# Query and key products by seven: order of the tiles in a bank, order of the jobs, place of the attention

## The chip, the cores and the metric

The kernel runs on one core of a Trainium2 chip. The metric is the device time of one execution in microseconds, the median of several runs. A core has engines with a queue of instructions each: TensorE (PE in the profile; PEld is its weight load), VectorE (DVE), ScalarE (ACT), GpSimd (POOL) and SyncE (SP), which here only issues transfers between the chip's main memory and the core's working memory. An engine works through its queue in order; where an instruction needs another engine's result it waits for a semaphore, and everything behind it in its queue waits too. TensorE writes its results to PSUM, a memory of eight banks of 128 x 512 fp32 values, and VectorE and ScalarE read them from there.

## The reference

One layer of a hybrid decoder, 512 positions, width 1024, all in fp32:

```python
u = rmsnorm(x, ln1_g[i])
proj = u @ w_in[i]
q, k, v, pool_in, z, xbc, dt_raw, gate_pre = jnp.split(proj, split_idx, axis=-1)
y_a = dilated_attention_mixer(q, k, v, rel_bias) @ w_a[i]
y_b = pool_mixer(pool_in, pool_w[i], pool_scale[i]) @ w_b[i]
y_c = ssd_mixer(z, xbc, dt_raw, ssd_conv_w[i], ...) @ w_c[i]
merged = gates[:, :, 0] * y_a + gates[:, :, 1] * y_b + gates[:, :, 2] * y_c
x = x + merged @ w_o[i]
x = x + conv_ffn(rmsnorm(x, ln2_g[i]), ...)
return rmsnorm(x, final_g)
```

The attention has three groups of six heads of 64 columns; group 0 looks back without gaps, group 1 at every fourth position, group 2 at every sixteenth. The change concerns the queries and keys of group 1: 384 columns of `w_in` each, so two products of 512 x 1024 by 1024 x 384.

## The kernel before, in words

**Three products for one.** A product in fp32 is made of three: each operand is split into a high part (fp32r) and the remainder, and high by high, high by low and low by high are added in PSUM (`mm3`, L228). For the weights, ScalarE casts the high part (`wh`, L195) and VectorE subtracts it from the raw weights to get the low one (`wl`, L215). The matmuls that use `wl` come last in a tile.

**Jobs.** All work with weights is a list of jobs, written by hand in `program()` (L1473). A job has a load, a cast, a split and a body of matmuls. The main loop (L1684 on) does this before the body of job n: the split of the weights of n+1, the cast for n+2, the fetch for n+3. The cast is cut in two and its halves are issued in the body's steps. There are two buffers of raw weights, three of high parts, two of low parts. TensorE, VectorE, ScalarE and GpSimd do their instructions in the order of the program; SyncE's order is left to the scheduler of the framework, which may take a transfer that is ready ahead of one that is not.

**Steps.** `step()` (L156) issues the pending half of a cast and lets side work go on one piece: a list of waiting items, one taken up per step, among them the heads of the attention, which `attend(g)` (L725) puts there. An attention item does its scores in the step that takes it up, its softmax on VectorE and ScalarE, its transposes two steps later and its output product after that.

**Seven products for eight.** The product of group 1's queries and keys is cut in quarters (rows of the weights even and odd by blocks of 128, columns query and key; positions in two halves) and computed by seven quarter products of sums and differences instead of eight (`qk_sevens`, L647): one, two, five, three, six, seven, four. The sums of `u` are in `US`; the sums of weights are made on VectorE (`diff`, L338) in place: `W[0]` and `W[1]` are two quarters loaded on their own (L657), and `W[0]` becomes `W[0]` less one's weights, `W[1]` becomes `W[1]` less the new `W[0]`. Five takes its weights from `W[0]`, three and six from `W[1]`, one, two, seven and four have loads of their own.

A job of `qk_sevens` has three tiles c = 0, 1, 2 of 128 columns by 256 positions, 12 matmuls each. A bank of PSUM takes two such tiles: tiles 0 and 1 share a bank, tile 2 has the first half of a second one. X and Z (tag `sm`, four banks in all) and Y (tag `mm`) are pairs of banks. One writes X, two Y, five Z; three adds to Z, and six, seven and four add to X. After each tile its reader runs: a copy to working memory on ScalarE (L696 for one and five, L705 for six) or a sum on VectorE (L700 for two, L706 for six, L709 for seven); three is not read. The framework keeps two engines off the same bank: a matmul into one half waits for a read of the other half that was issued before it.

**The order around it.** Before the change the list runs: value product of groups 1 and 2, also by seven (`v_pair`, whose results SyncE copies into place, `vr<-v`, L624), then one gate job (two tiles of 512 positions), the seven query/key jobs, attention of group 1, one more gate job, and the six jobs (twelve tiles) of the convolution's input (`xbc_evac`, L901).

Of the kernel before, what the change touches and what calls it, by code (L numbers as in the profile page):

```python
# [13 lines left out]
OP = mybir.AluOpType  # L14
# [69 lines left out]
def trunk(ctx: ExitStack, tc, out, x, rel_bias, ln1_g, w_in, b_gate, w_a, pool_w, pool_scale, w_b,  # L84
# [3 lines left out]
    act, dve, pool, pe, sp = nc.scalar, nc.vector, nc.gpsimd, nc.tensor, nc.sync  # L88
# [19 lines left out]
    def T(name, dt=F32, shape=(P, S)):  # L108
        return big.tile(list(shape), dt, name=name, tag="t")
# [228 lines left out]
    def diff(out, a, b):  # L338
        dve.tensor_tensor(out, a, b, OP.subtract)  # L339
        return out  # L340
# [70 lines left out]
    def side_u(j):  # L411
        if j in QUARTER:
            two, half = QUARTER[j]
            return [(uh[:, 2 * p + two, half], ul[:, 2 * p + two, half]) for p in range(4)]
        return [US[j, p] for p in range(4)]
# [154 lines left out]
    def grouped(ap, g):  # L570

        return ap.rearrange("p (r j) -> p r j", r=4)[:, :, ::-1]
# [4 lines left out]
    def plain(ap, g):  # L577
        return ap if g == 0 else ap.rearrange("p (r j) -> p r j", r=4)
# [68 lines left out]
    def qk_sevens(g):  # L647

        cols = (C_Q + 384 * g, C_K + 384 * g)
        q = lambda two, h: w_in[:, cols[h]:cols[h] + 384].rearrange(  # L650
            "(k two p) c -> two p k c", two=2, p=P)[two]
        W, X, Z, Y, r1, r5 = [], {}, {}, {}, {}, {}

        def load():
            for h in range(2):
                W.append(ypool.tile([P, 4, S], F32, name="w3", tag="xs")[:, :, :384])
                sp.dma_start(W[h], q(h, 1))  # L657

        def at(banks, c):
            return banks[c // 2][:, (c % 2) * 256:(c % 2) * 256 + 256]  # L660

        def half(which, c, hi):
            if (which, g, c) not in QK:
                QK[which, g, c] = T(f"{which}{g}")
            t = QK[which, g, c]
            t = grouped(t, g) if which == "q" else plain(t, g)
            return t[:, :, 64 * hi:64 * hi + 64]

        def turned_(ap):
            return ap.rearrange("p (j r) -> p r j", r=4)  # L670

        def job(source, j, banks, name, use, form=None):
            def body(ws):
                wh, wl = ws
                parts = side_u(j)
                for c in range(3):
                    fresh = name is not None
                    if fresh and c % 2 == 0:
                        banks[c // 2] = (MM if banks is Y else SM)(name)
                    cs = slice(c * P, (c + 1) * P)  # L680
                    mm3(at(banks, c), lambda k: wh[:, k, cs], lambda k: wl[:, k, cs],
                        lambda k: parts[k][0], lambda k: parts[k][1], range(4),
                        fresh and c % 2 == 0, True, again=not fresh or c % 2 == 1)
                    use(c)
                    if c != 1:
                        step()
            new = Job([source] if source is not None else [], 4, 384, body)
            new.form = form
            if source is None:
                new.load = lambda: None  # L690
            return new

        def keep(r, name, banks, scale):
            def use(c):
                r[c] = T(name)[:, :256]
                act.mul(r[c], at(banks, c), scale)  # L696
            return use

        def p2(c):
            dve.scalar_tensor_tensor(half("q", c, 0), turned_(at(Y, c)), 0.125, turned_(r1[c]),  # L700
                                     OP.mult, OP.add)

        def p6(c):
            r = T("r2")[:, :256]
            act.copy(r, at(X, c))  # L705
            dve.tensor_tensor(half("k", c, 0), turned_(at(Z, c)), turned_(r), OP.add)  # L706

        def p7(c):
            dve.tensor_tensor(half("k", c, 1), turned_(at(X, c)), turned_(r5[c]), OP.add)  # L709

        def p4(c):
            act.mul(half("q", c, 1), turned_(at(X, c)), 0.125)

        one = job(q(0, 0), "A11", X, "p1", keep(r1, "r1", X, 0.125))
        one.then = lambda: diff(W[0], W[0], one.raw)
        two = job(q(1, 0), "A12", Y, "p2", p2)
        five = job(None, 1, Z, "p5", keep(r5, "r5", Z, 1.0), lambda: W[0])
        three = job(None, 4, Z, None, lambda c: None, lambda: W[1])
        three.then = lambda: diff(W[1], W[1], W[0])
        six = job(None, 2, X, None, p6, lambda: W[1])  # L720
        seven = job(q(0, 0), 3, X, None, p7, lambda: diff(seven.raw, W[1], seven.raw))
        four = job(q(1, 0), "A22", X, None, p4, lambda: diff(four.raw, four.raw, W[1]))
        return load, [one, two, five, three, six, seven, four]

    def attend(g):  # L725
        nm, ls = both[:, :, :HEADS], both[:, :, 32:]
# [265 lines left out]
    btok, cb, prev, done = {}, {}, {}, set()  # L992
# [166 lines left out]
    def gate_jobs(b, lo=0, hi=8):  # L1159
        def evac(m, ps):  # L1160
            s = SG[b, lo + m] = T("sg")
            o = o_bg + 8 * b + lo + m
            act.activation(s, ps, AF.Sigmoid, bias=col[:, o:o + 1])  # L1163
            if b == 1:
                dve.tensor_tensor(MG[lo + m], MG[lo + m], s, OP.mult)

        return jobs_a(w_in, C_GATE + b * D + lo * P, hi - lo, uhk, ulk, KD, evac)
# [305 lines left out]
    def program():  # L1473
        yield from jobs_a(w_in, C_POOL, 8, uhk, ulk, KD, pool_evac)
        yield Call(lambda: waiting.append(rows_of_bias()))
        yield from v_jobs(0)
        yield from qk_jobs(0)
        yield from pool_out_job()
        yield Call(lambda: attend(0))
        yield Call(lambda: waiting.insert(3, ssd_prep()))  # L1480
        for i, job in enumerate(branch_jobs(1, w_b, YB, 8, more=range(7))):
            if i == 3:
                yield Call(lambda: running.extend(after(p, sums_of_u(p)) for p in range(4)))
            yield job
        load, pair = v_pair()
        yield Call(load)
        yield from gate_jobs(1, 0, SPLIT)
        load, keys = qk_sevens(1)
        for i, job in enumerate(pair):
            yield job  # L1490
            if i == 5:
                yield Call(load)
        yield from gate_jobs(1, SPLIT, SPLIT + 2)
        yield from keys
        yield Call(lambda: attend(1))
        yield from gate_jobs(1, SPLIT + 2)
        yield from jobs_a(w_in, C_XBC, 12, uhk, ulk, KD, xbc_evac)
        yield Call(ssd_start)
        yield from qk_jobs(2)
        yield Call(lambda: attend(2))  # L1500
        yield Call(lambda: fill([after(2, combine())]))
        yield from gate_jobs(0)
        many = {"a": branch_jobs(0, w_a, AO, 3), "g": gate_jobs(2),
                "Z": z_jobs(0), "z": z_jobs(1)}
        for token in MIX:
            if token in many:
                yield next(many[token])
            else:
                yield Call(lambda i=int(token): waiting.append(y_norm(i)))
        yield Call(finish)  # L1510
        yield from branch_jobs(2, w_c, YT, 8, last=True)
        yield Call(load_x1)
        for pair in range(2):
            for h in range(2):
                yield from wo_jobs(pair, h)
            if pair == 0:
                yield Call(ff_cols)
        first, between, _ = sevens_down(0)
        second_, last_, opened = sevens_down(1, keep=True)
        extra = {EARLY + i: between[w] for i, w in enumerate(  # L1520
            ("two", "one", "five", "three", "six", "seven", "four"))}
        extra.update({LATE + i: last_[w] for i, w in enumerate(("two", "one", "five", "six"))})
        for i, job in enumerate(up_jobs()):
            yield job
            if i == EARLY - 3:
                yield Call(first)
            if i == LATE - 1:
                yield Call(second_)
            if i in extra:
                yield extra[i]  # L1530
        yield Call(lambda: fin.setdefault("g", grow(final_g)))
        yield Call(finish)
        yield from down(last_, opened)
# [87 lines left out]
    for tb in range(2):  # L1621
        s0, s1, v, sq, r, rt = (small(n, [P, 1]) for n in ("s0", "s1", "v", "sq", "r", "rt"))
# [25 lines left out]
    r = rstd_of(ss, 2, D)  # L1648
# [68 lines left out]
SPLIT = 4  # L1717
# [33 lines left out]
```

## Time and profile before

| what | us |
|---|---|
| median of 3 runs | 1046.34 (1044.05 to 1047.76) |
| the profiled execution, its own time | 1045.46 |
| its span, first to last instruction | 1043.5 |
| TensorE busy | 1024.7 |
| VectorE busy | 690.7 |
| ScalarE busy | 475.1 |
| the seven query/key jobs, first to last matmul's start | 247.26 to 287.64 in the span |

How to read it: an engine's busy time is the sum of its instructions. A row of the timeline has the start and the length of one instruction or of a few alike, the engine, the line of the kernel, the operation, what it writes and reads, its shape and count; in brackets how long the engine had stood before it and whose result ended that. Matmuls are pipelined: one's length overlaps the next, so the distance of two starts says what a matmul takes. Names of tiles are shown without digits: p1, p2 and p5 are all `p`. Rows with "SPq" are issues of transfers.

### The profile page before, as it was taken

To read this page: it belongs to the slowest core of one execution; us is meant where nothing else is said; L and a number is where in the kernel's file an instruction comes from. 1 tells how busy PE (TensorE), PEld (TensorE's weight loads), DVE (VectorE), ACT (ScalarE), POOL (GpSimd) and SP (SyncE) were. 2 spreads that over 40 slices of the span, in tenths; PEclk is the share of its full clock that TensorE was granted. 3 is DMA by queue.
4 is the path that set the end of the run, shared out by engine and by line. 5 is a ranking of instruction groups with operands and counts; after the bars stand their busy time and mean duration, and the time that the engine had idled before them with its cause. 6 is when DMAs were issued, how large, how long until landed. Compare 5 with 4: busy or idle time off the path is not lost.

```text
span 1043.5 us, 13347 instructions
## 1 busy us (share of the span) xinstructions
PE 1024.7 (98%) x5312; PEld 864.2 (83%) x5312; DVE 690.7 (66%) x921; ACT 475.1 (46%) x778; POOL 149.4 (14%) x125
## 2 busy tenths in 40 slices
PE   9999999998899999999999999999999999999997
PEld 9998878897788878888888888898888888888885
DVE  5563566685647657767677755767677776666775
ACT  5432544443355354565564333545445344453342
POOL 1670000000000004310134500001110000111120
PEclk9999999999999999999999999999999999999999
DMA  7444312045232235342244535443223324323142
GB/s 262 138 126 138 115 48 74 31 122 161 83 120 81 81 101 162 96 149 79 81 131 140 173 104 210 164 142 110 93 81 122 119 72 173 121 81 121 61 142 81
DMA packets 115996, 122.34 MB, mean 117 GB/s; under 512 B 5315, under 2 KB 98310, under 8 KB 115935
## 3 DMA queue, kind: packets, MB, share of 16 engines
q1 hardware_dynamic: 115343, 120.64, 35.8%
q8 instruction: 42, 0.69, 0.3%
q10 hardware_dynamic: 592, 0.86, 0.2%
q14 instruction: 19, 0.16, 0.0%
HBM read 117.69 MB, written 2.22 MB: 115 GB/s over the span
## 4 chain that ended last, share of the span: by engine, by line
PE 92%; DVE 3%; ACT 2%; DMA 1%; issue 1%; SPq 1%; ACTq 0%; DVEq 0%
PE pa L234 34%; PE pu L234 22%; PE pb L234 10%; PE p L234 9%; PE pqk L234 6%; PE pa L1602 2%; PE ps L748 1%; PE pu L1404 1%; DVE wl L215 1%; PE ppw L234 1%; PE pt L776 1%; PE po L789 1%; PE py L1074 1%; DMA xin<-in_x_dram 1%; ACT wh L195 1%
## 5 line engine op out<-in xcount | busy, mean ns | idle before, releaser
L215 DVE TENSOR_TENSOR wl<-raw,wh 128x2048 fp32r<-128x2048 f32 (+3 forms) x96 | 218.5, 2278 | 49.9 <-ACT wh L195 42.3
L195 ACT CAST wh<-raw 128x1024 fp32r<-128x1024 f32 (+3 forms) x190 | 189.5, 1017 | 66.0 <-DVE raw L339 36.4
L1265 DVE SCALAR_TENSOR_TENSOR hc<-pu,fcol,hc 128x510 f32<-128x510 f32 x88 | 65.8, 747 | 61.2 <-ACT hc L1262 59.6
L234 PE MATMUL pa<-uh,wh 128*128 128x512 f32 x384 | 98.6, 399 | 0.0
L234 PE MATMUL pa<-ul,wh 128*128 128x512 f32 x384 | 94.9, 389 | 0.0
L234 PE MATMUL pa<-uh,wl 128*128 128x512 f32 x384 | 94.9, 389 | 0.0
L234 PEld LDWEIGHTS pa<-ul,wh 128*128 128x128 f32 x384 | 72.1, 188 | 15.2
L234 PEld LDWEIGHTS pa<-uh,wl 128*128 128x128 f32 x384 | 72.1, 188 | 15.0
L234 PE MATMUL pu<-uh,wl 128*128 128x512 f32 (+1 forms) x352 | 83.7, 380 | 0.0
L234 PE MATMUL pu<-uh,wh 128*128 128x512 f32 (+1 forms) x352 | 83.6, 379 | 0.0
L234 PE MATMUL pu<-ul,wh 128*128 128x512 f32 (+1 forms) x352 | 83.5, 379 | 0.0
L234 PEld LDWEIGHTS pa<-uh,wh 128*128 128x128 f32 x384 | 70.2, 188 | 14.6 <-issue 0.7
L234 PEld LDWEIGHTS pu<-uh,wl 128*128 128x128 f32 x352 | 64.1, 188 | 12.7 <-DVE wl L215 0.3
L234 PEld LDWEIGHTS pu<-ul,wh 128*128 128x128 f32 x352 | 64.2, 188 | 12.4
L234 PEld LDWEIGHTS pu<-uh,wh 128*128 128x128 f32 x352 | 64.1, 188 | 12.4
L1270 POOL TENSOR_TENSOR hc<-hc 128x512 f32<-128x512 f32 x22 | 30.4, 1381 | 278.9 <-DVE hc L1265 243.9
L1262 ACT ACTIVATE hc<-pu,fcol,fcol 128x512 f32<-128x512 f32 x40 | 31.2, 780 | 82.6 <-PE pu L234 82.3
L1036 POOL TENSOR_TENSOR xd<-xc,dec 128x512 f32<-128x512 f32 x6 | 6.4, 1062 | 341.6 <-DVE xc L1030 322.7
L769 ACT ACTIVATE sb<-sb,both 128x128 f32<-128x128 f32 (+1 forms) x72 | 30.1, 419 | 29.1 <-DVE both L766 18.9
L1163 ACT ACTIVATE sg<-pa,col 128x512 f32<-128x512 f32 x24 | 16.5, 687 | 50.4 <-PE pa L234 43.7
L1267 ACT ACTIVATE hc<-hc 128x512 f32<-128x512 f32 x22 | 13.9, 632 | 42.7 <-DVE hc L1265 42.6
L912 DVE SCALAR_TENSOR_TENSOR xs<-pa,col,xs 128x509 f32<-128x509 f32 (+2 forms) x24 | 18.0, 749 | 17.0 <-ACT xs L908 16.5
(376 smaller groups left out, 1867.0 us busy)
## 6 DMA issues: line engine op xcount, KB each, us to landing
raw<-in_w_in_dram SPq DMA_DIRECT2D x25, 1024.0 KB
raw<-in_ffn_w_up_dram SPq DMA_DIRECT2D x22, 1024.0 KB
raw<-in_ffn_w_down_dram SPq DMA_DIRECT2D x11, 1024.0 KB
raw<-in_w_o_dram SPq DMA_DIRECT2D x8, 1024.0 KB
raw<-in_w_in_dram SPq DMA_DIRECT2D x14, 512.0 KB
raw<-in_w_in_dram SPq DMA_DIRECT2D x8, 768.0 KB
raw<-in_w_b_dram SPq DMA_DIRECT2D x4, 1024.0 KB
al<-ad SPq DMA_DIRECT2D x16, 256.0 KB
```

Of the source, the lines that this page charges most:

```text
L195: act.copy(job.high[:, :, o], job.raw[:, :, o])
L215: (eng or dve).tensor_tensor(l[:, :, o], job.raw[:, :, o], h[:, :, o].bitcast(F32), OP.subtract)
L234: pe.matmul(ps, l, r, start=first and n == 0, stop=last and n == total - 1, skip_group_check=again)
L748: pe.matmul(pss[i][:, o:o + w * P], q[r, n * P:(n + 1) * P], k[r, kb * P:(kb + w) * P], start=True, stop=True)
L769: act.activation(sb[:, off:off + w * P], sb[:, off:off + w * P], AF.Exp, bias=nm[:, n, h:h + 1], accum_out=ls[:, n, h:h + 1])
L912: dve.scalar_tensor_tensor(t[:, sh:], ps[:, :S - sh], col[:, o_cw + 12 * k + m:o_cw + 12 * k + m + 1], t[:, sh:], OP.mult, OP.add)
L1163: act.activation(s, ps, AF.Sigmoid, bias=col[:, o:o + 1])
L1262: act.activation(t, ps, AF.Identity, bias=ff["c1"][:, ff["b"] + m:ff["b"] + m + 1], scale=fw(2, m))
L1265: dve.scalar_tensor_tensor(t[:, sh:], ps[:, :S - sh], fw(k, m), t[:, sh:], OP.mult, OP.add)
L1267: act.activation(t, t, AF.Silu)
L1270: pool.tensor_tensor(a, a, t, OP.mult)
L1602: pe.matmul(first[2 * n + j][:, lo:hi], a[:, k, j * P:(j + 1) * P], b[:, k, lo:hi], start=a is wh and b is uh and k == 0, stop=a is wl and ...
```

## The change

In the body of a job of `qk_sevens`, tiles 0 and 1 are computed, then both are read, then a step is taken; tile 2 is computed and read and a second step is taken. Before, each tile was read right behind its matmuls and the first step came after tile 0. In seven, each tile is first copied to working memory by ScalarE, and VectorE's sum reads the copy. The jobs come as one, five, two, three, then the gate job, six, the second gate job, seven, four. Attention of group 1 starts behind four as before, but no gate job follows it: the convolution's jobs do.

```diff
@@ qk_sevens, body of a job
                         fresh and c % 2 == 0, True, again=not fresh or c % 2 == 1)
-                    use(c)
-                    if c != 1:
+                    if c:
+                        for done in (0, 1) if c == 1 else (2,):
+                            use(done)
                         step()
@@ qk_sevens, the reads
         def p7(c):
-            dve.tensor_tensor(half("k", c, 1), turned_(at(X, c)), turned_(r5[c]), OP.add)
+            r = T("r7")[:, :256]
+            act.copy(r, at(X, c))
+            dve.tensor_tensor(half("k", c, 1), turned_(r), turned_(r5[c]), OP.add)
@@ qk_sevens, what it returns
-        return load, [one, two, five, three, six, seven, four]
+        return load, [one, five, two, three], [six, seven, four]
@@ program
-        load, keys = qk_sevens(1)
+        load, begun, ended = qk_sevens(1)
         for i, job in enumerate(pair):
             yield job
             if i == 5:
                 yield Call(load)
+        yield from begun
         yield from gate_jobs(1, SPLIT, SPLIT + 2)
-        yield from keys
+        yield ended[0]
+        yield from gate_jobs(1, SPLIT + 2)
+        yield from ended[1:]
         yield Call(lambda: attend(1))
-        yield from gate_jobs(1, SPLIT + 2)
         yield from jobs_a(w_in, C_XBC, 12, uhk, ulk, KD, xbc_evac)
```

## The prediction

> **What bounds the kernel now.** I read the page's head and its chain first, then who waits for whom on TensorE, then the stretch that the change touches. On the page the first two lines are the span and TensorE's busy time, the third is the end of the chain.
>
> ```profile
> span 1043.5 us, 13347 instructions
> PE 1024.7 (98%) x5312; PEld 864.2 (83%) x5312; DVE 690.7 (66%) x921; ACT 475.1 (46%) x778; POOL 149.4 (14%) x125
> ...
> PE 92%; DVE 3%; ACT 2%; DMA 1%; issue 1%; SPq 1%; ACTq 0%; DVEq 0%
> ```
>
> TensorE carries the end: whatever delays its queue delays the kernel, other engines count only where TensorE waits for them. All its waits between 236 and 400 us are these:
>
> ```profile
> PE p L234 <- ACT r L696: 2.3, 3, 1.5
> PE p L234 <- DVE q L700: 2.1, 1, 2.1
> PE p L234 <- DVE k L709: 1.7, 1, 1.7
> PE p L234 <- ACT r L705: 1.6, 2, 1.1
> PE pcb L1005 <- ACT xcv L1093: 1.0, 1, 1.0
> PE p L234 <- ACT q L712: 0.5, 1, 0.5
> ```
>
> Columns: total, times, longest. Five of the six rows, 8.2 us in eight waits, are matmuls of the tiles p1 to p5 waiting for a reader in the group-1 query/key product, the function edited. By stretch (length, then busy time of TensorE, its weight loads, VectorE, ScalarE): one gate job, the seven products, the next gate job.
>
> ```profile
> 236.34:247.26 10.92, 10.92 (x49) 9.02 (x49) 6.18 (x6) 2.16 (x3) 0.00 (x0) 1.00 0.64 204
> 247.26:287.64 40.38, 32.24 (x253) 30.61 (x252) 23.55 (x20) 16.34 (x27) 0.00 (x0) 1.00 0.32 102
> ```
>
> The gate job is dense. The products are not, and TensorE's rows in order of time show how (start, length, operation, idle before and its releaser):
>
> ```profile
> 250.34 0.74 PE L234 MATMUL p<-uh,wh 128*128 128x256 f32 x4 [1.49 <-ACT r L696]
> ...
> 251.87 0.64 PE L234 MATMUL p<-uh,wh 128*128 128x256 f32 x4
> ...
> 253.31 0.64 PE L234 MATMUL p<-uh,wh 128*128 128x256 f32 x4
> ...
> 276.25 0.74 PE L234 MATMUL p<-sbh,wh 128*128 128x256 f32 x4 [1.15 <-ACT r L705]
> ...
> 279.63 0.74 PE L234 MATMUL p<-sbh,wh 128*128 128x256 f32 x4 [1.69 <-DVE k L709]
> ...
> 284.67 0.74 PE L234 MATMUL p<-uh,wh 128*128 128x256 f32 x4 [0.47 <-ACT q L712]
> ```
>
> A tile of 12 matmuls unhindered takes 253.31 - 251.87 = 1.44 us. The tile at 250.34 is the second half of a bank whose first half ScalarE was reading: it waited though the columns are different. The tile at 251.87, another bank, did not. So the half just written is read while the other half's matmuls stand still, in six of the seven jobs (three has no read), and two more waits stand where a job begins on a bank read late.
>
> **The change, part by part.** *Both halves first, then both reads.* The seven jobs hold 21 tiles; 21 x 1.44 = 30.24 us of the 40.38. The excess, 10.14 us, is what waits cost in start times: the 8.2 us of wait rows, and the restart after each (0.74 instead of 0.64 us for its first four, and a drained array). In the new order no read lies between the two tiles of a bank, so all six mid-bank waits go. I take off 10.14 and add back what is late next.
>
> Three ways of counting differ here. The stretch less busy matmul time gives 40.38 - 32.24 = 8.14 us to win, the starts give 10.14; I take the starts, since they include the restarts. The Trainium skill, "Perfetto Trace Analysis", section "Identifying the Most-Contended Engine", says that matmul busy time misleads, because pipelined instructions look smaller in the trace, and that weight-load time is the better measure; by it the window is 40.38 - 30.61 = 9.77 us, nearer to the starts, and the forecast would be 0.4 us slower.
>
> *The two waits at a job's start* (six's read before seven, 1.15 us; five's before three). Five and three now have two between them, 4.3 us of other banks; six and seven have a gate job of 10.92 us between. Cost nothing, covered by those; without the cover about the old 1.15.
>
> *Seven's copy.* Three more ScalarE reads of 128x256 from PSUM, priced by their likes:
>
> ```profile
> L705 ACT COPY r<-p x3: 364/372/374, 271.5 to 276.1; 128x256 f32<-128x256 f32 x3
> L709 DVE TENSOR_TENSOR k<-p,r x3: 605/624/626, 279.0 to 282.8; 128x256 f32<-128x256 f32 x3
> ```
>
> That is 3 x 0.37 = 1.1 us on an engine 16.34 us busy in 40.38. VectorE's three additions stay at most at 0.62 each. Seven and four remain neighbours on one bank: seven's two reads take 0.7 us and run under seven's third tile (1.44 us), so four starts unhindered; were ScalarE inside a cast (0.83 us, below) when they are due, four would wait about 0.1. Bounds 0 and the old 1.7; I take 0, as the casts are queued behind the reads.
>
> *The step after the first tile moves behind the second.* A step issues half a weight cast for the job two ahead, which now enters ScalarE's queue behind two reads, one tile (1.44 us) later. That matters only where a split is already short, next.
>
> *The order: one, five, two, three, gate, six, gate, seven, four.* One now follows the value product directly, at 236.34 instead of 247.26, and five follows one. This is the new price; VectorE, ScalarE and SyncE in that place:
>
> ```profile
> 235.28 2.28 DVE L215 TENSOR_TENSOR wl<-raw,wh 128x2048 fp32r<-128x2048 f32 x1
> 237.48 1.01 DVE L619 TENSOR_TENSOR v<-r,pb 128x384 f32<-128x384 f32 x2
> 243.08 1.76 DVE L215 TENSOR_TENSOR wl<-raw,wh 128x1536 fp32r<-128x1536 f32 x1 [4.59 <-ACT wh L195]
> 244.76 1.75 DVE L339 TENSOR_TENSOR w<-w,raw 128x1536 f32<-128x1536 f32 x1
> ...
> 229.56 3.47 ACT L195 CAST wh<-raw 128x768 fp32r<-128x768 f32 x4 [3.55 <-DVE raw L339]
> 241.48 1.57 ACT L195 CAST wh<-raw 128x768 fp32r<-128x768 f32 x2 [8.45 <-DMA raw<-in_w_in_dram]
> 247.86 0.83 ACT L195 CAST wh<-raw 128x768 fp32r<-128x768 f32 x1 [4.23 <-DMA raw<-in_w_in_dram]
> ...
> 219.51 0.37 SPq L183 DMA_DIRECT2D raw<-in_w_in_dram  x1
> 220.13 5.66 SPq L624 DMA_DIRECT2D vr<-v  x8
> 227.82 2.04 SPq L657 DMA_DIRECT2D w<-in_w_in_dram  x2
> 230.55 5.99 SPq L624 DMA_DIRECT2D vr<-v  x8
> 236.64 0.53 SPq L183 DMA_DIRECT2D raw<-in_w_in_dram  x1
> 237.27 4.93 SPq L624 DMA_DIRECT2D vr<-v  x8
> 242.30 0.53 SPq L183 DMA_DIRECT2D raw<-in_w_in_dram  x1
> 242.93 5.68 SPq L624 DMA_DIRECT2D vr<-v  x8
> ```
>
> One's weights take the raw buffer that the gate's had, so they are fetched at 219.51 and cast by 233. VectorE splits them at 235.28 where it split the gate's: 1.76, done 237.04. TensorE uses the low parts last, after 8 of 12 matmuls: 236.34 + 0.96 = 237.30. In time, by 0.26.
>
> Five's weights are W[0] less one's. W[0] and W[1] are issued by 229.86; a fetch of the same 768 KB took 241.48 - 236.64 = 4.84 us, so they are there by 234.7. The subtraction runs 236.96 to 238.7, the two value additions behind it end at 239.7 (nobody waits for them but the copies vr, needed by attention much later), ScalarE casts by 238.77 + 1.57 = 240.34, VectorE splits by 242.15. TensorE reaches five at 236.34 + 4.32 = 240.66, its low parts at 241.62. Short by 0.55, and with a restart 0.8 us. This is the one term I add; its ends are 0, if VectorE comes to the split half a microsecond sooner, and 2.1, the longest wait the stretch has shown.
>
> Two's weights come in the buffer free when the last value job is split, issued at 236.64 and landed 241.48 as one's did. ScalarE's cast of them, in two halves around one's third read, ends near 243.5; split by 245.3. TensorE, now 0.8 late, starts two at 245.8: in time. Three: cast behind five's reads by 247.1, split by 248.9, needed at 250.1. The gate job's fetch comes next in SyncE's queue at 242.30 and has until 254.4. From there each product has a gate job's 10.92 us of slack.
>
> *Attention moves behind four.* The gate job that hid its first two items now runs before, so its seven entries begin in the convolution's first tile, with 12 steps instead of 14 before the scan. The last entry is taken at step 7 and works at step 9: it fits. VectorE there:
>
> ```profile
> 302.72 2.28 DVE L215 TENSOR_TENSOR wl<-raw,wh 128x2048 fp32r<-128x2048 f32 x1
> 306.32 2.31 DVE L912 SCALAR_TENSOR_TENSOR xs<-pa,col,xs 128x509 f32<-128x509 f32 x3 [1.32 <-ACT xs L908]
> 308.55 0.68 DVE L762 TENSOR_TENSOR sb<-ps,b 128x512 f32<-128x512 f32 x1
> 309.27 0.69 DVE L766 TENSOR_REDUCE both<-sb 128x4 f32<-128x512 f32 x1
> 309.87 0.68 DVE L777 COPY sb<-pt 128x512 f32<-128x512 f32 x1
> ```
>
> A tile's share is 2.31 + 2.28/2 + 0.68 + 0.69 + 0.68/2 = 5.2 us, against 10.92/2 = 5.46 us of its matmuls and the attention's own beside them. It fits, narrowly; cost nothing, and without that cover about one copy per tile, 0.3 us each.
>
> **Sum.** 10.14 - 0.8 = 9.3 us. The profiled execution is listed at 1045.46 us, so 1036.1; the median before is 0.9 higher than that execution. I forecast 1036.5.
>
> **The rivals.** *Two's fetch falls behind the third group of copies* (SyncE takes it at 242.30 instead of 236.64). For it: the copies are ahead of it in the code. Against: at 219.51 a fetch was issued ahead of copies that the code puts first, whichever was ready earlier going first, and two's buffer is free before those copies' data. Price: landed 247.1, cast and one's third read 0.83 + 0.38 + 0.83 to 249.2, split to 250.9, where the low parts were due at 246.8; with a restart some 4.3 us. Time 1040.8.
>
> *The stretch turns out paced by ScalarE and VectorE.* VectorE's 23.55 us and the chain cast, split, difference stay, in 31 us instead of 40.38; then each wait removed returns before a weight and the time stays near 1045. For it, the narrow margins above. Against, the value product just before:
>
> ```profile
> 207.20:236.34 29.14, 29.14 (x169) 29.14 (x168) 24.38 (x25) 13.63 (x20) 0.00 (x0) 1.00 0.38 116
> ```
>
> There VectorE is busy 24.38 of 29.14 us and TensorE never stops.
>
> *Slower: W[0] and W[1] are issued late.* In the old order one's weights, not W[0], came last, so nothing shows that W is early enough when five follows one. Issue to usable split is 4.84 + 1.75 + 1.57 + 1.76 = 9.92 us; needed at 241.62. Issued behind the third group of copies, 242.30, five waits 10.6 us and the gain is gone (1045.9). Behind the fourth, 248.6, it waits 16.9: 1045.5 - 10.1 + 16.9 = 1052.3. It decides from an issue at 241.8 on. Against it, the row at 227.82, with the same buffers free at the same time. The Trainium skill, "TensorE: Matmul & The Clock Gate", section "What's actually happening", adds that after an idle window of about 3.4 us the clock falls to half for as long: an estimate from it is 1.7 us on top; no wait in this stretch is long enough to show it, and the granted clock in its rows is 1.00.
>
> **How the numbers follow.** Forecast 0.70, range 1034 to 1038.5 (0 to 2 us of small waits, and the runs' spread); late fetch of two 0.16; no gain 0.06; slower 0.08. The range 1033.5 to 1042 holds the first two. About 0.3% (3 us) can be told from no change: faster 0.86, same 0.06, slower 0.08.
>
> **What would show it.** After the value product, tiles p run 1.44 us apart with no wait for r, q or k; one short wait for wl or wh near 241 to 242; the stretch from 236.34 to the end of four and both gate jobs is about 53 us; W is issued before the second group of copies. I am wrong if TensorE waits for wh or wl for several us among one, five, two and three, if new waits for k or r appear between seven and four, or if attention's transposes wait for VectorE.

## The result, and the profile after

The changed kernel takes 1034.84 us, the median of 5 runs (1034.7 to 1035.51), against 1045.85 (1044.05 to 1047.76, 5 runs) before: a ratio of 0.9895 with a 95% interval of 0.988 to 0.9909, 11 us less. The profiled execution took 1034.7 us with a span of 1033.0.

The page's head and its chain, which is TensorE's by 93%:

```profile
span 1033.0 us, 13348 instructions
PE 1022.2 (99%) x5312; PEld 863.1 (84%) x5312; DVE 690.9 (67%) x921; ACT 473.3 (46%) x779; POOL 149.6 (14%) x125
...
PE 93%; DVE 3%; ACT 2%; DMA 1%; issue 1%; ACTq 0%; SPq 0%; DVEq 0%
```

TensorE's waits between 200 and 400 us (total, times, longest) are down from six rows to two, and the second is the wait that the prediction put there:

```profile
PE pcb L1008 <- ACT xcv L1096: 1.0, 1, 1.0
PE p L234 <- DVE wl L215: 0.5, 1, 0.5
```

It stands in five, after eight of its first tile's twelve matmuls; before and behind it the tiles run 1.44 us apart, and seven and four follow each other without a gap (TensorE in order of time, changed kernel):

```profile
240.13 0.64 PE L234 MATMUL p<-sal,wh 128*128 128x256 f32 x4
241.23 0.74 PE L234 MATMUL p<-sah,wl 128*128 128x256 f32 x4 [0.46 <-DVE wl L215]
...
280.88 0.64 PE L234 MATMUL p<-sbh,wh 128*128 128x256 f32 x4
...
282.32 0.64 PE L234 MATMUL p<-sbh,wh 128*128 128x256 f32 x4
...
283.76 0.64 PE L234 MATMUL p<-uh,wh 128*128 128x256 f32 x4
```

To compare kernels with different orders I use one length, called the stretch: from the end of the value product to the end of the seven products and both gate jobs, without attention. Its ends are starts of matmuls, the last that of the first one behind it. Where the second gate job lies behind four, its 10.92 us are added. In these two rows (length, then busy time of TensorE, weight loads, VectorE and ScalarE) stand the whole stretch of the changed kernel and, of the kernel before, the part up to the end of four:

```profile
235.34:288.08 52.74, 52.28 (x349) 48.28 (x349) 33.51 (x29) 22.23 (x37) 0.00 (x0) 1.00 0.44 141
```

```profile
236.34:287.64 51.30, 43.16 (x301) 39.63 (x301) 29.73 (x26) 18.50 (x30) 0.00 (x0) 1.00 0.39 124
```

Before it is 51.30 + 10.92 = 62.22 us, after 52.74: 9.48 us less. Without any wait it would be 30.24 + 2 x 10.92 = 52.08. The spans differ by 10.5 us, though. The other 1.0 us lies ahead of the change: the value product ended at 236.34 and now ends at 235.34; the last experiment looks at whether that is chance. From the end of the stretch on nothing changed: the convolution's tiles and the attention take 363.65 - 288.08 = 75.57 us where they took 374.10 - 287.64 - 10.92 = 75.54 (first matmul of the group-2 queries; before, then after):

```profile
374.10 1.98 PE L234 MATMUL pqk<-uh,wh 128*128 128x512 f32 x8
```

```profile
363.65 1.98 PE L234 MATMUL pqk<-uh,wh 128*128 128x512 f32 x8
```

### The profile page after: what moved, and what is told of

Its sections match the earlier page's. It is cut to its first block, busy times and chain, and to the rows that moved or that the text cites. A ratio compares the mean times of both kernels' runs of the same rounds, so it can differ in the third digit from the quotient of the medians.

```text
span 1033.0 us, 13348 instructions
## 1 busy us (share of the span) xinstructions
PE 1022.2 (99%) x5312; PEld 863.1 (84%) x5312; DVE 690.9 (67%) x921; ACT 473.3 (46%) x779; POOL 149.6 (14%) x125
## 4 chain that ended last, share of the span: by engine, by line
PE 93%; DVE 3%; ACT 2%; DMA 1%; issue 1%; ACTq 0%; SPq 0%; DVEq 0%
PE pa L234 35%; PE pu L234 21%; PE pb L234 10%; PE p L234 10%; PE pqk L234 6%; PE pa L1607 2%; PE ps L751 1%; PE pu L1407 1%; DVE wl L215 1%; PE ppw L234 1%; PE pt L779 1%; PE po L792 1%; PE py L1077 1%; ACT wh L195 1%; DMA xin<-in_x_dram 1%; PE pyo L1084 1%
```

## The experiments

The theory to be tested: the waits are matmuls kept off a bank while its other half is read, so grouping the reads is the change's whole gain. Its main rival: the gate jobs between the products give ScalarE and VectorE time to read promptly, so the order is the gain. Three parts can be had one by one: the grouped reads, seven's copy, the order.

### Grouped reads alone

Old order, VectorE reads seven's tiles from the bank; only this differs from the kernel before. It moves the step too: half a cast now enters ScalarE's queue behind the reads of tiles 0 and 1 and no longer between them.

```diff
-                    use(c)
-                    if c != 1:
+                    if c:
+                        for done in (0, 1) if c == 1 else (2,):
+                            use(done)
                         step()
```

> The kernel before with one edit: tiles 0 and 1 of a bank are computed, then both read. Order of jobs, place of the gate jobs and seven's read by VectorE stay as before. The stretch is counted from the start of the first gate job or product to the end of the seven products and both gate jobs without the attention: 62.2 us before, 52.7 after the whole change, 52.1 without any wait. Theory 1 (the waits are matmuls that must not touch a bank while its other half is read): all six mid-bank waits go; what is left is the handover of X from seven to four, where VectorE, behind four's split, reads late: about 2.3 us of wait. Stretch 54.7, some 7.5 us faster than before, about 1038.3. Theory 2 (the gain comes from the order, which gives ScalarE and VectorE time between the products): waits of 1 to 2 us stay between the jobs, gain 3 us or less, about 1043.

Measured: 1037.55 us (1036.53 to 1038.3), ratio 0.992 (0.9905 to 0.9934). One wait is left in the list for the stretch, the handover of X from seven to four. The kernel before had none there; it comes with the grouped reads, as expected:

```profile
274.98 0.74 PE L234 MATMUL p<-uh,wh 128*128 128x256 f32 x4 [1.89 <-DVE k L710]
```

```profile
235.81:279.40 43.59, 41.66 (x301) 39.34 (x301) 29.77 (x26) 17.91 (x30) 0.00 (x0) 1.00 0.44 141
```

The stretch is 43.59 + 10.92 = 54.51 us, 7.7 us less than before. All six mid-bank waits are gone with the order untouched; the first theory holds, the second has nothing left to explain but the last 1.9 us. In the kernel before, the longest of them, 2.06 us, ended at 256.97, with the read of two's first tile, which stood behind a split on VectorE:

```profile
254.65 1.76 DVE L215 TENSOR_TENSOR wl<-w,wh 128x1536 fp32r<-128x1536 f32 x1 [2.85 <-ACT wh L195]
256.32 0.59 DVE L700 SCALAR_TENSOR_TENSOR q<-p,r 128x256 f32<-128x256 f32 x1
```

The two waits at a job's start, 0.34 and 1.15 us, are gone as well, and ScalarE's rows put that down to the step's move. Before, six's second tile was read behind the half cast that the step had issued, and that cast waited for VectorE; now the reads of tiles 0 and 1 go first and only the third tile's stands behind the cast. ScalarE before, and then with grouped reads, where seven starts at 268.33:

```profile
275.10 0.83 ACT L195 CAST wh<-raw 128x768 fp32r<-128x768 f32 x1 [3.18 <-DVE raw L339]
275.84 0.64 ACT L705 COPY r<-p 128x256 f32<-128x256 f32 x2
```

```profile
267.09 0.65 ACT L706 COPY r<-p 128x256 f32<-128x256 f32 x2 [0.39 <-PE p L234]
270.25 0.83 ACT L195 CAST wh<-raw 128x768 fp32r<-128x768 f32 x1 [2.51 <-DVE raw L339]
270.99 0.36 ACT L706 COPY r<-p 128x256 f32<-128x256 f32 x1
```

Seven's third tile starts 0.2 us late for it (271.41 in place of 271.21), and no more. Grouped reads without the step's move were not run. VectorE shows why four waits: its reads of seven (L710) stand behind the split of four's weights.

```profile
272.12 1.76 DVE L215 TENSOR_TENSOR wl<-raw,wh 128x1536 fp32r<-128x1536 f32 x1
273.80 1.66 DVE L710 TENSOR_TENSOR k<-p,r 128x256 f32<-128x256 f32 x3
```

### Grouped reads and the copy, old order

As the last, and in seven:

```diff
-            dve.tensor_tensor(half("k", c, 1), turned_(at(X, c)), turned_(r5[c]), OP.add)
+            r = T("r7")[:, :256]
+            act.copy(r, at(X, c))
+            dve.tensor_tensor(half("k", c, 1), turned_(r), turned_(r5[c]), OP.add)
```

> As reads_only, and seven is copied by ScalarE before VectorE adds; order of jobs and gates as before the change. Theory 1: the handover to four shrinks from 2.3 to about 0.1 us, and since one still stands behind a gate job, five's split is in time: no wait is left, the stretch is 52.2 to 52.5 us, as short as that of the whole change (52.7) or shorter; the new order is worth nothing once the reads are grouped. About 1036. Theory 2 (the gates between the jobs are needed): waits of 2 us or more remain, 1038 or more.

Measured: 1034.8 us (1034.46 to 1035.2), ratio 0.9895 (0.9879 to 0.9912): the whole gain, without the new order. TensorE waits for nothing in the stretch that the list of waits shows:

```profile
235.18:276.76 41.58, 41.55 (x302) 39.36 (x302) 29.08 (x26) 18.26 (x32) 0.00 (x0) 1.00 0.44 138
```

41.58 + 10.92 = 52.50 us, 0.24 less than with the new order. The second theory's waits of 2 us or more do not show.

### The order alone

Each tile is read behind its matmuls, VectorE reads seven from the bank, and the jobs come in the new order. Against the changed kernel:

```diff
-                    if c:
-                        for done in (0, 1) if c == 1 else (2,):
-                            use(done)
+                    use(c)
+                    if c != 1:
                         step()
@@ seven: as before the change
```

> The new order of jobs and gates alone: each tile is read right behind its matmuls, as before the change, and seven's read is VectorE's. Theory 1: all six mid-bank waits stay, each at least 0.63 us (ScalarE's read when idle, with restart), and two grow, since ScalarE is casting five's weights when one's first tile is to be read (about 3 us) and VectorE splits three's weights and takes a difference before it reads two's (about 2.9 us): in all some 8.8 us of the 10.1, stretch about 61, time 1044 to 1045. Theory 2: with gates between the jobs the reads are prompt; waits of 0.6 us each, stretch 56 or less, time 1040 or less.

Measured: 1050.14 us (1050.02 to 1050.3), ratio 1.0041 (1.0026 to 1.0056): slower than before. The stretch is 303.34 - 235.39 = 67.95 us. TensorE's rows of its first product, and of two:

```profile
239.77 1.22 PE L234 MATMUL p<-uh,wh 128*128 128x256 f32 x4 [2.79 <-ACT r L696]
240.79 1.05 PE L234 MATMUL p<-ul,wh 128*128 128x256 f32 x4
...
254.64 1.22 PE L234 MATMUL p<-uh,wh 128*128 128x256 f32 x4 [3.85 <-DVE q L700]
...
295.35 0.71 PE L234 MATMUL p<-sbh,wh 128*128 128x256 f32 x4 [2.53 <-DVE k L709]
```

The mid-bank waits are all there and three have grown. The first theory said that they stay, but its stretch of 61 us and its 1044 to 1045 us are missed by 7 and by more than 5: it had named only two that grow, at about 3 and 2.9 us, and it had left something out: behind the waits of 2.79 and 3.85 us four matmuls start 0.85 to 1.02 us before the next four, where 0.48 is usual. The granted clock (the number behind GpSimd's column) says why:

```profile
239.70:242.00 2.30, 2.23 (x10) 2.23 (x11) 1.52 (x1) 0.85 (x2) 0.00 (x0) 0.50 0.33 94
...
254.60:257.00 2.40, 2.36 (x11) 2.36 (x12) 0.00 (x0) 0.00 (x0) 0.00 (x0) 0.50 0.00 0
257.00:260.00 3.00, 3.00 (x16) 3.00 (x16) 0.62 (x1) 0.64 (x1) 0.00 (x0) 0.50 0.00 0
260.00:264.30 4.30, 4.30 (x38) 4.30 (x37) 2.83 (x2) 0.92 (x2) 0.00 (x0) 0.99 0.06 6
```

It fell to half for 3.4 us at the end of the first of these waits, and for 6.8 us from within the second. The second theory's 1040 us or less is out. Of the 67.95 - 52.08 = 15.9 us of excess the waits of the list are 10.8; the other 5 are restarts (some 0.25 for each of six waits) and the clock. Behind the wait of 2.53 us it did not fall.

### The whole change without the copy

> The whole change without seven's copy: VectorE reads seven's tiles from the bank, as before. Theory 1: with a gate job ahead of seven, VectorE reads behind four's split about 0.3 to 0.5 us after four is due; stretch 53.2, time within 0.1% of the changed kernel (1034.8 to 1035.5). Rival (the copy is what frees the bank in time): a wait of 1.7 us as in the kernel before, and 1036.5 or more.

Only the copy's lines are taken back. Measured: 1035.06 us (1034.65 to 1035.59), ratio 0.9897 (0.9882 to 0.9912). The stretch is 288.22 - 235.01 = 53.21 us, and four waits for VectorE:

```profile
283.83 0.71 PE L234 MATMUL p<-uh,wh 128*128 128x256 f32 x4 [0.19 <-DVE k L710]
```

So the copy and the order are two cures for the same wait of 1.9 us, and either takes away nearly all of it; the rival's 1.7 us did not come. With grouped reads the stretch is 54.51 with neither, 52.50 with the copy, 53.21 with the order, 52.74 with both. The order's 52.74 and 53.21 hold 0.6 us that it causes itself, five's wait.

### The second gate job behind four again

```diff
         yield from begun
         yield from gate_jobs(1, SPLIT, SPLIT + 2)
-        yield ended[0]
-        yield from gate_jobs(1, SPLIT + 2)
-        yield from ended[1:]
+        yield from ended
         yield Call(lambda: attend(1))
+        yield from gate_jobs(1, SPLIT + 2)
```

> The changed kernel with its second gate job back behind four, so that six, seven and four follow each other and the first two attention items have the gate job's steps again. Theory: six's reads, seven's difference and four's are done while six's and seven's matmuls run; no wait among them, attention no different: stretch and time as the changed kernel's within 0.3 us (52.7; 1034.8). Rival (jobs on the same banks must be set apart by a gate job): four or seven waits 1 to 2.5 us on X, 1036 to 1037. Second rival (attention without the gate's steps crowds VectorE): this kernel is faster than the changed one by over 0.3 us.

Measured: 1034.81 us (1033.87 to 1035.1), ratio 0.989 (0.9863 to 0.9917). The stretch is 277.30 - 235.45 + 10.92 = 52.77 us, five's 0.5 us the only wait of the products. Neither rival shows. With the copy, no gate job is needed between jobs on the same bank. Attention does not mind where it starts: from the end of the stretch to the group-2 queries it is 363.79 - 277.30 - 10.92 = 75.57 us again, so the 0.6 us by which the changed kernel beside it was slower (1035.43) are not attention's.

### Two behind one, in the new place

The changed kernel with `[one, two, five, three]` for `[one, five, two, three]`.

> The changed kernel with the old order one, two, five, three. Theory: two's raw weights land at about 240.1 in that trace and two is due at 239.65; its cast and split follow, so TensorE waits about 1.6 us for the cast and 2 us for the split, restarts included, and five's 0.6 us goes: 3.1 us slower than the changed kernel, about 1038. Rival (the scheduler fetches two earlier, or the cast is in time): no difference.

Measured: 1038.12 us (1037.15 to 1039.77), ratio 0.9925 (0.9897 to 0.9953), 2.7 us slower than the changed kernel run beside it. Two's weights landed late, its cast began at 241.56 in the profiled execution, and TensorE's rows are:

```profile
242.45 0.74 PE L234 MATMUL p<-uh,wh 128*128 128x256 f32 x4 [2.38 <-ACT wh L195]
243.02 0.64 PE L234 MATMUL p<-ul,wh 128*128 128x256 f32 x4
244.98 1.22 PE L234 MATMUL p<-uh,wl 128*128 128x256 f32 x4 [1.32 <-DVE wl L215]
```

The two waits are where the expectation had them, 3.7 us in all, and the row at 244.98 again starts at the slower clock. (The profiled execution is the slowest of the four, 1039.77.) Five in second place is right if one follows the value product directly.

### The first gate job ahead of one again

The changed kernel with `gate_jobs(1, SPLIT, SPLIT + 2)` moved ahead of `begun`; six then follows three directly.

> The changed kernel with its first gate job ahead of one again: gate, one, five, two, three, six, gate, seven, four. Theory: five's split is in time, since the gate job hides the difference and the cast; six follows three directly, its cast and split ready 1.5 us ahead of need. No wait left in the stretch: 52.1 us, 0.6 faster than the changed kernel, less than the times can tell. Rival (six needs a gate ahead of it): a wait of 1 us or more for wh or wl before six.

Measured: 1035.36 us (1035.08 to 1035.45), ratio 0.9896 (0.9865 to 0.9928). TensorE does not stop once:

```profile
234.89:286.94 52.05, 52.05 (x349) 48.24 (x349) 33.61 (x29) 21.65 (x36) 0.00 (x0) 1.00 0.43 138
```

The stretch is 0.7 us shorter than the changed kernel's, which the times can't show: they are the same within the spread. No version tried beats the changed kernel by a measurable amount.

### W[0] twice

The forecast's slower case as an experiment: W[0] is fetched a second time into the same place.

```diff
                 sp.dma_start(W[h], q(h, 1))
+                if h == 0:
+                    sp.dma_start(W[h], q(h, 1))
```

> The changed kernel with W[0] fetched twice into the same place, the second fetch waiting for the first; nothing else differs. It tests the price of the forecast's slower case: from issue to usable split 9.9 us, needed at 240.6 in the changed kernel's trace. If the second fetch is issued as soon as the first has landed, at about 231, it lands at 236 and five waits no longer than now (0.6 us). If SyncE issues it behind the second group of copies, at about 235.3, five's split is ready at 245.2 and five waits about 4.7 us instead of 0.6, and the clock falls behind that wait as it did behind one of 3.85 us in the kernel with the new order alone: 4 us for the wait and about 2.5 us for the clock, 1041.

Measured: 1042.13 us (1040.47 to 1042.99), ratio 0.9959 (0.9942 to 0.9976), 7 us slower than the changed kernel. SyncE's issue, VectorE's difference and split, and TensorE's waits:

```profile
235.92 0.59 SPq L659 DMA_DIRECT2D w<-in_w_in_dram  x1
```

```profile
241.18 1.76 DVE L339 TENSOR_TENSOR w<-w,raw 128x1536 f32<-128x1536 f32 x1 [5.22 <-DMA w<-in_w_in_dram]
...
244.65 1.76 DVE L215 TENSOR_TENSOR wl<-w,wh 128x1536 fp32r<-128x1536 f32 x1 [0.78 <-ACT wh L195]
```

```profile
PE p L234 <- ACT wh L195: 4.2, 1, 4.2
PE p L234 <- DVE wl L215: 1.1, 1, 1.1
```

From issue to usable split it is 244.65 + 1.76 - 235.92 = 10.5 us, against 9.92 worked out. The waits are 5.3 us where they were 0.5; restarts and the clock, at 0.50 for 6.8 us about the second wait, are the rest of the 7 us. So the slower rival's mechanism was real and its way of pricing a late W about right, for W[0] alone and an issue at 235.92; its condition, a late issue, did not come about (226.82 in the changed kernel).

### Both kernels once more

> The changed kernel once more. The first 235 us hold the same program in both kernels, yet in the two traces the value product ended 1.0 us earlier in the changed one, because x landed earlier at the start. If that is chance between executions, the end of the value product lies anywhere between 235 and 237 us here and the times of repeated runs spread by about 1 us; if the change causes it, it is 235.3 again in every kernel with the new order and 236.3 in the kernels with the old one.

The changed kernel: 1035.43 us (1035.0 to 1035.97), stretch 288.40 - 235.66 = 52.74 us, the same to the hundredth, while the value product ended 0.32 us later than in the first profile. In all profiles it ended between 235.01 and 235.66 us where the new order follows it and between 234.89 and 236.34 where the gate job does, as in the old one. The two ranges overlap and neither of the expected values recurs, which speaks for chance.

> The kernel before once more. In the runs so far its times go from 1043.85 us at a mean granted clock of 0.999 to 1049.15 at 0.996, while the changed kernel stays between 1034.7 and 1036.0 at 0.998 to 0.999; the trace of before shown is one at 0.999. Theory: one of the longer waits of the seven products (1.5 to 2.1 us) lets TensorE's clock fall in some executions, which makes the stretch 1 to 4 us longer than 40.4; the traces of such a run show a granted clock of about 0.5 for some us behind it. Rival: the clock falls elsewhere (the start, the scan), and the change only happened to meet better executions: the stretch from the first product to the end of four is 40.4 us in every profile of this kernel, whatever its time.

> As before_again: a further profile of the kernel before, to have one with a mean clock of 0.997 or below beside one of 0.999. In the first the stretch of the seven products is longer by what its time is longer; in the second it is 40.4 us.

The kernel before: 1045.72 us (1043.91 to 1048.66, 9 runs), ratio to itself 0.9996 (0.9979 to 1.0013); one more profile at 1045.79. In both new profiles the stretch is longer than the 62.22 us of the first: 63.2 and 63.1 us (41.35 and 41.25 from one to the end of four, against 40.38). Two things differ. The wait in one is shorter, 0.96 and 0.84 us for 1.49, which takes 0.5 and 0.65 us off. And behind the wait for two's read, 2.06 us in all three, the clock falls to half, so that two's last two tiles take 4.46 and 4.47 us in place of 2.98. The rows are 3.41 us each, for a reason given at the end; TensorE's busy time is the second number, the granted clock the third from the right. First profile, second, third:

```profile
252.22:255.63 3.41, 2.69 (x23) 2.48 (x21) 0.98 (x1) 2.35 (x5) 0.00 (x0) 1.00 0.84 259
255.63:259.05 3.42, 2.08 (x17) 2.08 (x18) 1.63 (x3) 0.45 (x1) 0.00 (x0) 1.00 0.00 1
```

```profile
252.26:255.67 3.41, 1.35 (x13) 1.15 (x11) 2.27 (x2) 2.50 (x4) 0.00 (x0) 1.00 0.57 206
255.67:259.08 3.41, 3.41 (x16) 3.41 (x17) 0.46 (x1) 0.00 (x0) 0.00 (x0) 0.50 0.00 0
```

```profile
252.60:256.01 3.41, 1.35 (x11) 1.15 (x10) 2.27 (x2) 2.33 (x4) 0.00 (x0) 1.00 0.58 206
256.01:259.42 3.41, 3.41 (x17) 3.41 (x17) 0.62 (x1) 0.00 (x0) 0.00 (x0) 0.50 0.00 0
```

Between its first rise, some 7 us from the start, and the last matmuls the clock falls nowhere else in the three profiles, so the rival (it falls elsewhere) is out. The last expectation was met only in part: both new profiles have a mean clock of 0.997, so the pair is made with the first one, and their stretches are longer by 0.9 to 1.0 us while their times are longer by only 0.3, since their value products ended 0.8 and 0.5 us earlier.

## Why the prediction was right, point by point

- **What bounds the stretch, and which waits go.** Right. Grouped reads alone took away all six mid-bank waits, and the stretch lost 7.7 us.
- **The two waits at a job's start, and the step.** Right that they go, wrong in why. The prediction had them covered by the jobs put between, and 1.15 us without that cover; with grouped reads in the old order, which has no such cover, seven starts without a wait and only its third tile is 0.2 us late. By ScalarE's rows it is the step's move that removed them, which the prediction took to matter only where a split is short.
- **10.14 us to win, counted by starts.** Right for that execution: the kernel with the first gate job ahead of one again, which has no wait, is 52.05 us where the count said 52.08. Busy matmul time would have given 8.1. Weight loads gave 9.77, and so the rule of the Trainium skill ("Perfetto Trace Analysis", "Identifying the Most-Contended Engine") agrees with the trace here in that they come nearer than busy matmuls (9.77 and 8.14 for 10.14).
- **Five's wait, 0.8 us.** Right in place and cause; 0.46 of wait and 0.62 us with its restart.
- **Seven's copy at nothing.** Right: no wait between seven and four. What the prediction did not see is that grouped reads bring a new wait there, 1.89 us, that either the copy or the order removes it, and that the order alone has a price, five's wait.
- **The order of SyncE's queue.** Half right. W and two's weights went ahead of the copies, as argued. The gate's weights did not: issued at 246.59 instead of 242.30, behind 16 copies, they were cast from 251.72 for a job that began at 253.32. The wait stayed away by about 0.6 us, not by 6.

```profile
235.31 0.53 SPq L183 DMA_DIRECT2D raw<-in_w_in_dram  x1
235.94 10.54 SPq L624 DMA_DIRECT2D vr<-v  x16
246.59 46.33 SPq L183 DMA_DIRECT2D raw<-in_w_in_dram  x8
```

- **Attention behind four at nothing.** Right: 75.57 us against 75.54, and no difference with the gate job put back.
- **The size.** 9.3 us were forecast; the stretch gave 9.48 between the two profiles, and the medians 11.0. The term that was sized too small is the 10.14, since it was read from one execution in which the clock stayed whole. The sentence that no wait in the stretch is long enough for the clock to fall was wrong: behind the wait of 2.06 us it fell in two of three profiles of the kernel before, at about 1.5 us each, so removing the waits also removes that. Of the 40 runs of the kernel before that were made beside the experiments, 12 have a mean clock of 0.999 and a median of 1044.6 us, and 28 have one of 0.997 or less and a median of 1046.5; the changed kernel's nine runs have a median of 1035.0. So without the fall of the clock the gain is about 9.6 us, near the forecast, and what is beyond that goes with the clock; where it fell in the runs without a profile is not on record. What is left between single executions lies at the start: the first value product, 180 us ahead of the change and with the same program before it, begins at 59.65, 58.88 and 59.16 us in the three profiles of the kernel before, and at 58.68 and 58.95 in the two of the changed one.
- **The rivals.** Two's fetch was not late (235.31). The pace of VectorE and ScalarE did not show, with 33.51 of 52.74 us busy. The late W was priced by fetching W[0] twice.

## What to carry to other kernels

Where two tiles share a PSUM bank, write both before either is read; a read between them stops TensorE for the length of the read and of whatever stands ahead of it in the reader's queue. When the next job needs the same bank, let the reader with the shorter queue empty it, issue no work that can wait ahead of its reads, and look for these cures before reordering jobs: here a copy of 1.1 us on an engine with room did the work of a new order, and the new order without grouped reads made the kernel slower. An order has its price where it shortens the way from a load to its first use, and that price can be worked out from the rows of before to a few tenths of a microsecond.

## What the runs showed of the hardware

TensorE's clock fell to half behind waits much shorter than I had taken as safe, though not behind all of them. At half, four 256-column matmuls took 0.85 us instead of 0.48. The traces also show when it falls. In each of the 13 profiles the times at which the granted clock changes lie whole multiples of 3.413 us apart (in the kernel with the new order alone, 10.240 and 6.827 us). So it is set on beats of 3.413 us, which a wait does not move, and here it stayed at half for one beat or two. Counting how long TensorE stands idle, by the profile, within each beat at the full clock sorts every case, in all profiles from the clock's first rise on: behind a beat with 2.06 us or more of idle time it fell, behind one with 1.73 us or less it never did, and no beat lay between.

| wait | profile | most idle time in one beat, us | clock |
|---|---|---|---|
| 2.06 us, two | kernel before, second and third | 2.06 | fell |
| 2.06 us, two | kernel before, first | 1.33 | stayed |
| 2.79 us, one | order alone | 2.61 | fell |
| 3.85 us, two | order alone | 2.46 | fell |
| 2.53 us, seven | order alone | 1.38 | stayed |
| 2.38 and 1.32 us, two | two behind one | 2.20 | fell, within the second wait |
| 4.20 us, five | W[0] twice | 2.52 | fell 0.9 us behind the wait |
| 1.89 us, four | grouped reads alone | 1.69 | stayed |

In the rows of the three profiles above, the edge of a beat at 255.63 cuts the first one's wait (254.91 to 256.97) in two, and the others' lie whole inside one beat. Which of the two an execution meets is luck, and that was the luck of the first profile. The limit lies between 1.73 and 2.06 us of idle time in 3.413 us for these matmuls; other kernels were not tried. The Trainium skill, "TensorE: Matmul & The Clock Gate", section "What's actually happening", puts the fall behind an idle window of about 3.4 us; the half clock and the 3.4 us agree with these rows, but the window need not be idle throughout. The clock makes the kernel before vary from run to run (1043.3 to 1049.85 us in the last comparison) where the changed one keeps within 1.3 us.
